# Four CA batches on VectorE and four on GpSimd, two buffers each for CA's products and for the turned E

## The chip, the cores and the metric

The kernel runs on one core of a Trainium2 chip. The metric is the device time of one execution in microseconds; the time shown is the median of three runs. The profile is of one further execution.

The core has five instruction streams that run side by side and meet at semaphores: TensorE (PE, matmuls; its weight loads are PEld), VectorE (DVE), ScalarE (ACT), GpSimd (POOL) and SyncE (SP), which here only issues DMAs. ACT issues DMAs too. Each stream executes in the order in which it was written: an instruction that waits holds back all that stands behind it on its engine.

## The reference, cut to what matters

One layer of a hybrid backbone over 512 latent tokens and 256 context tokens, all in float32. One input projection feeds three branches, which are merged by sigmoid gates and projected, and a squared-ReLU MLP follows. The change lies in branch B, a bidirectional S5 state-space layer with 32 groups of 16 channels and 64 complex states:

```
h_f = diag_scan(lam_bar[0], s5_drive(ux, b_bar[0])) + exp(lam_dt[0] * steps) * h0_f
h_b = diag_scan(lam_bar[1], flip(s5_drive(ux, b_bar[1]), 1)) + exp(lam_dt[1] * steps) * h0_b
y = real(einsum('blgp,gnp->blgn', h_f, c_mat[0]) + einsum('blgp,gnp->blgn', h_b, c_mat[1]))
y = y + d_skip * u;  g = gelu(y);  yb = (g @ w_glu_a) * sigmoid(g @ w_glu_b)
```

The kernel runs the scan over blocks of eight steps. For that it needs, per group, the input matrix times powers of lambda (the program calls it E), the output matrix times powers of lambda (CA) and the lag kernel of a block (KT). They depend on parameters only and are made at run time.

## The kernel before, in words

**Units.** The large matrices stream from HBM as 1 MB pieces `raw` through two buffers, each of which holds two halves. A half is split into a rounded part and a rest: ACT writes `wh` (L173), VectorE writes `wl` (L176). Three matmuls (L99, L100, L101) per 128 rows use them. One half is one *unit* of PE work. The units stand in a fixed list: xa, cg, xb (four each), uc (four, the context's S5 input, 256 columns), then ga, ga, cv four times, eight gb, eight gc, and then q, k, v. `slot` (L1130) takes a unit and, between its parts, pulls small pieces of the side work from generators (`pump`, L1111). A SyncE load of `raw` waits until both halves of the buffer before it are split (L144 behind L176).

**E.** `gen_s5e` (L424) makes E in eight batches of four groups. Per batch GpSimd does six TENSOR_TENSOR instructions (L422 products, L458 and L467 sums) into `e1`; PE makes the lag matmuls `kps` (L436), ACT copies them to `kev` (L437); PE turns E in `etps` (L443), ACT copies that to `et` (L445) and sends it to DRAM (E_d, L446). After the last batch SyncE writes KT_d from `kev` in 15 DMAs (L484).

**CA.** `gen_s5c` (L487) makes CA in eight batches of six instructions: two products and a difference, two products and a sum (L497 to L499; the products are in the helper `prod`, L422). Batches 0 to 4 run on VectorE, 5 to 7 on GpSimd. The result `c1` goes to DRAM by SyncE (C_d, L501). `c1` and the second product `tc` have one buffer each, the input `cb` (loaded by ACT's queue, L491) two.

**S5B.** `gen_s5b` (L720) follows when E and CA are done: its buffers lie where those of CA lay, so GpSimd's first instruction (IOTA, L618) and the first loads of `et` wait for the last C_d transfer. It has eight batches. Batch q: 32 state matmuls `stps` (L666, L667; `et` and `u` come from DRAM), VectorE rotates by `tb` (L677, L678), GpSimd combines (L683, L684), VectorE scans (L691, eight instructions) and rotates back (L697, L698), GpSimd combines `h` (L703 to L706), PE makes the output `yps` (L713, L715; needs `ks` from KT_d and `ca` from C_d), ACT copies it to `y`. `rot1` of a batch stands behind the scan of the batch before on VectorE.

**What sets the order.** The program does not fix the order of an engine by hand. The framework sorts the instructions of each engine by priority with its own timing model while the kernel is built; two pieces of code that are pumped side by side can come out interleaved. A change of buffer counts therefore moves instructions on every engine.

Of the kernel before, what the change touches and what calls it, by code (L numbers as in the profile page):

```python
# [9 lines left out]
F32 = mybir.dt.float32  # L10
# [65 lines left out]
def trunk(tc, xT, ctxT, cond, condT, vecs, wst, s5p, s5bc, dmat, biasA, outT):  # L76
# [3 lines left out]
    V, S, P, PE = nc.vector, nc.scalar, nc.gpsimd, nc.tensor  # L80
# [23 lines left out]
    with es:  # L104
# [11 lines left out]
        def pa(name):  # L116
            return pp.tile([128, 1024], F32, tag="a", bufs=2, name=name)
# [300 lines left out]
        def prod(eng, out, mat, cf, b):  # L418
            shp = [128, 4, 8, 16]
            m4 = mat[:, :, None, :].to_broadcast(shp)  # L420
            c4 = s5["CF"][cf][:, 4 * b:4 * b + 4, :, None].to_broadcast(shp)
            eng.tensor_tensor(out.rearrange("p (g s n) -> p g s n", g=4, s=8), m4, c4, op=MUL)  # L422

        def gen_s5e(pool):  # L424
            kev = pool.tile([128, 2, G, 16], F32, name="kev")

            def loadbc(b):
                t = pool.tile([128, 512], F32, tag="bc", bufs=2, name=f"bc{b}")
                nc.scalar.dma_start(t[:, 0:384], s5bc[b][:, 0:384])
                return t  # L430

            def lags(b, e1, cm):
                kps = pa(f"kps{b}")[:, :128].rearrange("p (g m) -> p g m", g=4)
                for g in range(4):
                    for c in range(2):
                        PE.matmul(kps[:, g], e1[:, c, 128 * g:128 * g + 128], cm[:, 4 * c + g], start=c == 0, stop=c == 1)  # L436
                S.copy(kev[:, :, 4 * b:4 * b + 4].rearrange("p e g m -> p g e m"), kps.rearrange("p g (e m) -> p g e m", e=2))  # L437

            def turned(b, e1):
                ps = pa(f"etps{b}").rearrange("p (a m) -> p a m", a=8)  # L440
                for g in range(4):
                    for c in range(2):
                        PE.transpose(ps[:, 2 * g + c], e1[:, c, 128 * g:128 * g + 128], ident)  # L443
                et = pool.tile([128, 8, 128], F32, tag="et", bufs=1, name=f"et{b}")
                S.copy(et, ps)  # L445
                nc.scalar.dma_start(E_d[b], et)  # L446

            bc, old = loadbc(0), None
            for b in range(9):
                if b < 8:  # L450
                    nxt = loadbc(b + 1) if b < 7 else None
                    B = bc[:, 0:128].rearrange("p (c g n) -> p c g n", c=2, g=4)
                    cm = bc[:, 128:384].rearrange("p (a m) -> p a m", a=8)
                    e1 = pool.tile([128, 2, 512], F32, tag="e1", bufs=2, name=f"e1{b}")
                    ta = pool.tile([128, 512], F32, tag="ta", name=f"ta{b}")
                    prod(P, e1[:, 0], B[:, 0], "cr", b)
                    prod(P, ta, B[:, 1], "nci", b)
                    P.tensor_tensor(e1[:, 0], e1[:, 0], ta, op=ADD)  # L458
                    yield
                if old is not None:  # L460
                    lags(b - 1, *old)
                    yield
                if b < 8:
                    ta = pool.tile([128, 512], F32, tag="ta", name=f"tb{b}")
                    prod(P, e1[:, 1], B[:, 0], "nci", b)
                    prod(P, ta, B[:, 1], "cr", b)
                    P.tensor_tensor(e1[:, 1], e1[:, 1], ta, op=SUB)  # L467
                    yield
                if old is not None:
                    turned(b - 1, old[0])  # L470
                    yield
                old = (e1, cm)
                bc = nxt

            kf0 = pool.tile([16, G, 16], F32, tag="bc", bufs=2, name="kf0")
            dmt = pool.tile([16, G, 16], F32, tag="bc", bufs=2, name="dmt")
            nc.scalar.dma_start(dmt, dmat)
            nc.sync.dma_start(kf0, kev[112:128, 0])
            yield
            V.tensor_tensor(kf0, kf0, dmt, op=ADD)  # L480
            V.tensor_tensor(kev[0:16, 1], kev[0:16, 1], kf0, op=ADD)
            for e, s in ((e, s) for s in range(8) for e in range(2) if e or s < 7):
                i = 16 * (7 * e + s)
                nc.sync.dma_start(KT_d[:, :, i:i + 16].rearrange("g n m -> n g m"), kev[16 * s:16 * s + 16, e])  # L484
            yield

        def gen_s5c(pool):  # L487
            for b in range(8):
                eng = V if b < 5 else P
                t = pool.tile([128, 128], F32, tag="cb", bufs=2, name=f"cb{b}")  # L490
                nc.scalar.dma_start(t, s5bc[b][:, 384:512])  # L491
                C = t.rearrange("p (c g n) -> p c g n", c=2, g=4)
                c1 = pool.tile([128, 2, 512], F32, tag="c1", bufs=1, name=f"c1{b}")
                yield
                for c, (x, y, o) in enumerate((("ar", "ai", SUB), ("ai", "ar", ADD))):
                    ta = pool.tile([128, 512], F32, tag="tc", name=f"tc{b}{c}")
                    prod(eng, c1[:, c], C[:, 0], x, b)  # L497
                    prod(eng, ta, C[:, 1], y, b)
                    eng.tensor_tensor(c1[:, c], c1[:, c], ta, op=o)  # L499
                    yield  # L500
                nc.sync.dma_start(C_d[b], c1)  # L501
                yield
# [660 lines left out]
        stc_cm.__exit__(None, None, None)  # L1163
        s5c_cm = tc.tile_pool(name="s5c", bufs=1, side="right")
        gcc = gen_s5c(s5c_cm.__enter__())
        gens.append(gcc)
        while ga_ in gens or gcc in gens or UNITS[i][0] != "ga":
# [306 lines left out]
```

## Time and profile before

| | |
|---|---|
| median of 3 runs | 1034.97 us (1033.2 to 1037.51) |
| profiled execution, its time | 1035.81 us |
| its span, first to last instruction | 1034.0 us (1.8 us lie around it) |
| PE busy | 993.0 us, 96% |
| DVE, ACT, POOL busy | 577.3, 379.8, 214.6 us |
| granted TensorE clock, mean | 0.982 |

[...] The page's slices show PE at 7 or 8 tenths in few places behind the start, and the clock at 8 or 9 tenths in some of the same slices.

### The profile page before, as it was taken

The numbers are of one execution on the slowest core, as the hardware profiler recorded it, in microseconds if no ns is written. First come the engines' busy times: TensorE is split into PE (matmuls) and PEld (weight loads), VectorE is DVE, ScalarE is ACT, GpSimd is POOL, SyncE is SP. The second block draws the span as 40 slices with busy tenths as digits, with TensorE's granted clock in tenths as the row PEclk, the third lists the DMA queues.
The fourth block names the chain that finished last, engine by engine and source line by source line (L and its number), as shares of the span: only waits on it lengthen the run. The fifth ranks groups of instructions, "written<-read, shape, count | busy, mean of one in ns | idle before, by whom it ended". The sixth has DMA issues, their size and how long they took to land.

```text
span 1034.0 us, 13596 instructions
## 1 busy us (share of the span) xinstructions
PE 993.0 (96%) x5386; PEld 815.8 (79%) x5386; DVE 577.3 (56%) x941; ACT 379.8 (37%) x611; POOL 214.6 (21%) x169
## 2 busy tenths in 40 slices
PE   7999997989899999999999999999999999999997
PEld 3468886778688787878877788998888888888887
DVE  4952899358781244676587895665432324443322
ACT  3234522332212233565465443444331213442311
POOL 3165654556752013310210200000000000000000
PEclk8999998999799999999999999999999999999999
DMA  9426345973547366443344574223232232232202
GB/s 367 171 95 207 124 133 194 243 253 128 173 137 223 129 246 233 137 146 107 127 144 153 190 257 151 82 84 120 82 122 82 82 119 85 82 123 82 82 1 82
DMA packets 64543, 149.38 MB, mean 144 GB/s; under 512 B 28864, under 2 KB 41152, under 8 KB 52064
## 3 DMA queue, kind: packets, MB, share of 16 engines
q1 hardware_dynamic: 47360, 137.90, 38.7%
q10 hardware_dynamic: 17120, 10.62, 3.6%
q8 instruction: 42, 0.69, 0.3%
q14 instruction: 21, 0.17, 0.0%
HBM read 130.16 MB, written 18.32 MB: 144 GB/s over the span
## 4 chain that ended last, share of the span: by engine, by line
PE 67%; DVE 13%; DMA 6%; POOL 6%; issue 3%; ACT 3%; SPq 1%; ACTq 0%; DVEq 0%; POOLq 0%
PE m L99 10%; PE m L100 10%; PE m L101 10%; DMA raw<-in_wst_dram 2%; DVE wl L176 2%; DVE v L691 2%; PE ops L846 2%; DMA C_d<-c 2%; PE wo L100 1%; PE wo L99 1%; PE wo L101 1%; PE st_a L515 1%; DVE fg L959 1%; PE ptps L831 1%; PE gc L99 1%
## 5 line engine op out<-in xcount | busy, mean ns | idle before, releaser
L176 DVE TENSOR_TENSOR wl<-raw,wh 128x1024 fp32r<-128x1024 f32 x144 | 193.6, 1344 | 218.8 <-ACT wh L173 213.9
L173 ACT CAST wh<-raw 128x1024 fp32r<-128x1024 f32 x144 | 151.1, 1050 | 300.4 <-PE m L100 151.1
L99 PE MATMUL m<-rg,wh 128*128 128x512 f32 (+1 forms) x480 | 184.2, 385 | 0.0
L101 PE MATMUL m<-rg,wl 128*128 128x512 f32 (+1 forms) x480 | 183.9, 384 | 0.0
L101 PEld LDWEIGHTS m<-rg,wl 128*128 128x128 f32 x480 | 90.1, 188 | 19.1
L99 PEld LDWEIGHTS m<-rg,wh 128*128 128x128 f32 x480 | 89.9, 188 | 18.7
L100 PE MATMUL m<-rg,wh 128*128 128x512 f32 (+1 forms) x256 | 96.4, 378 | 0.0
L1092 POOL TENSOR_TENSOR junk<-raw,silx 128x1024 f32<-128x1024 f32 x16 | 45.3, 2829 | 206.7 <-DMA raw<-in_wst_dram 198.0
L100 PE MATMUL m<-actl,wh 128*128 128x512 f32 x224 | 87.8, 392 | 0.0
L100 PEld LDWEIGHTS m<-rg,wh 128*128 128x128 f32 x256 | 48.0, 188 | 8.6
L100 PEld LDWEIGHTS m<-actl,wh 128*128 128x128 f32 x224 | 42.0, 187 | 9.8
L1047 DVE SCALAR_TENSOR_TENSOR fg<-m,mod,fg 128x512 f32<-128x512 f32 x14 | 10.5, 752 | 52.8 <-PE m L101 52.8
L691 DVE TENSOR_TENSOR_SCAN v<-r,v 128x96 f32<-128x96 f32 x64 | 29.5, 524 | 15.4 <-POOL v L683 15.4
L515 PE MATMUL st_a<-raw,cs 128*2 128x256 f32 x128 | 32.3, 407 | 5.5 <-DMA raw<-in_wst_dram 4.2
L92 ACT CAST rg<-relu 128x512 fp32r<-128x512 f32 (+1 forms) x36 | 20.3, 576 | 38.5 <-DVE relu L1040 38.5
L1096 DVE SCALAR_TENSOR_TENSOR jk<-raw,silx 128x1024 bf16<-128x1024 f32 x16 | 21.8, 1361 | 20.4 <-DMA raw<-in_wst_dram 20.3
L93 DVE TENSOR_TENSOR actl<-relu,rg 128x512 fp32r<-128x512 f32 (+1 forms) x36 | 22.3, 632 | 18.6 <-ACT rg L92 18.6
L100 PE MATMUL wo<-rg,wh 128*128 128x256 f32 (+1 forms) x104 | 31.8, 309 | 0.0
L99 PE MATMUL wo<-rg,wh 128*128 128x256 f32 (+1 forms) x104 | 31.8, 307 | 0.0
L101 PE MATMUL wo<-rg,wl 128*128 128x256 f32 (+1 forms) x104 | 31.5, 306 | 0.0
L515 PEld LDWEIGHTS st_a<-raw,cs 128*2 128x2 f32 x128 | 10.7, 89 | 24.8 <-issue 10.5
L846 PE MATMUL ops<-pt,v 128*64 128x128 f32 (+1 forms) x256 | 28.2, 293 | 1.2 <-ACT pt L833 1.2
(439 smaller groups left out, 2385.5 us busy)
## 6 DMA issues: line engine op xcount, KB each, us to landing
raw<-in_wst_dram SPq DMA_DIRECT2D x94, 1024.0 KB
E_d<-et ACTq DMA_DIRECT2D x8, 512.0 KB
C_d<-c SPq DMA_DIRECT2D x8, 512.0 KB
et<-E_d SPq DMA_DIRECT2D x8, 512.0 KB
ca<-C_d SPq DMA_DIRECT2D x8, 512.0 KB
raw<-in_wst_dram SPq DMA_DIRECT2D x4, 512.0 KB
u<-U_d SPq DMA_DIRECT2D x8, 256.0 KB
ks<-KT_d SPq DMA_DIRECT2D x32, 64.0 KB
```

The costliest lines, as they stand in the source:

```text
L92: S.copy(hi, src)
L93: (eng or V).tensor_tensor(lo, src, f(hi), op=SUB)
L99: PE.matmul(ps, a[0], b[0], start=start, stop=False)
L100: PE.matmul(ps, a[0], b[1], start=False, stop=False)
L101: PE.matmul(ps, a[1], b[0], start=False, stop=stop)
L173: S.copy(a, src)
L176: V.tensor_tensor(b, src, f(a), op=SUB)
L515: PE.matmul(ps, cs[:, kt], half(h)[:, 256 * (kt % 4):256 * (kt % 4) + 256], start=kt == 0, stop=kt == 7, skip_group_check=True)
L691: V.tensor_tensor_scan(v[:, g, c], r8, v[:, g, c], 0.0, op0=MUL, op1=ADD)
L846: PE.matmul(ops[r], v[:rows, vt, r], pt[:rows, h, t], start=t == 0, stop=t == 3, skip_group_check=True)
L1092: P.tensor_tensor(junk, half(h), silx, op=MUL)
L1096: V.scalar_tensor_tensor(jk, half(h), 1.0, silx, op0=MUL, op1=MUL, accum_out=modx[:, i:i + 1])
```

## The change

Three buffer counts and one limit. VectorE makes CA batches 0 to 3, GpSimd 4 to 7. `c1` and `tc` get two buffers each, and so does `et` in E.

```diff
@@ gen_s5e
-                et = pool.tile([128, 8, 128], F32, tag="et", bufs=1, name=f"et{b}")
+                et = pool.tile([128, 8, 128], F32, tag="et", bufs=2, name=f"et{b}")
@@ gen_s5c
-                eng = V if b < 5 else P
+                eng = V if b < 4 else P
-                c1 = pool.tile([128, 2, 512], F32, tag="c1", bufs=1, name=f"c1{b}")
+                c1 = pool.tile([128, 2, 512], F32, tag="c1", bufs=2, name=f"c1{b}")
-                    ta = pool.tile([128, 512], F32, tag="tc", name=f"tc{b}{c}")
+                    ta = pool.tile([128, 512], F32, tag="tc", bufs=2, name=f"tc{b}{c}")
```

The order on the engines follows from it. GpSimd, at the last batch of E (e_1300, ta_1301 and tb_1354 are batch 7 of E; c_1307, c_1421, c_1534 are CA batches 4, 5, 6); the rows marked + are new at their place:

```order
+L422 TENSOR_TENSOR c_1307<-cb_1305,CFar 128x512
+L422 TENSOR_TENSOR c_1307<-cb_1305,CFai 128x512
 L422 TENSOR_TENSOR ta_1301<-bc_1189,CFnci 128x512
+L422 TENSOR_TENSOR tc_1334<-cb_1305,CFai 128x512
+L422 TENSOR_TENSOR tc_1358<-cb_1305,CFar 128x512
+L499 TENSOR_TENSOR c_1307<-c_1307,tc_1334 128x512
+L499 TENSOR_TENSOR c_1307<-c_1307,tc_1358 128x512
 L422 TENSOR_TENSOR e_1300<-bc_1189,CFcr 128x512
 L422 TENSOR_TENSOR e_1300<-bc_1189,CFnci 128x512
```

Before, the six instructions of E's batch 7 stood together and CA began behind them. Now they lie among 12 products and 6 sums of CA batches 4 to 6: L458 of batch 7 comes behind the products of batch 5, L467 behind those of batch 6.

PE, at the second uc unit (uc_1426) where the lag matmuls of E's batch 7 (kps_1409) begin:

```order
-L436 MATMUL kps_1409<-bc_1189,e_1300 128x32 x3
 L99 MATMUL uc_1426<-rg_639,wh_1294 128x256
 L436 MATMUL kps_1409<-bc_1189,e_1300 128x32
 L100 MATMUL uc_1426<-rg_640,wh_1294 128x256
-L436 MATMUL kps_1409<-bc_1189,e_1300 128x32
-L101 MATMUL uc_1426<-rg_639,wl_1295 128x256
-L436 MATMUL kps_1409<-bc_1189,e_1300 128x32
-L99 MATMUL uc_1426<-rg_639,wh_1294 128x256
```

One of the eight kps stays there, behind the first matmul of the unit; the other seven, and seven of the eight etps of the batch, now stand behind the sixth matmul of the first ga unit.

PE, at the last S5B state batch (stps_2564) of the 8; before it comes in gb_2491, the first gb unit:

```order
-L100 MATMUL gb_2491<-rg_75,wh_2201 128x512
-L101 MATMUL gb_2491<-rg_73,wl_2202 128x512
-L99 MATMUL gb_2491<-rg_73,wh_2201 128x512
-L100 MATMUL gb_2491<-rg_75,wh_2201 128x512
 L666 MATMUL stps_2564<-u_2332,et_2399 64x96
 L667 MATMUL stps_2564<-u_2332,et_2399 64x96
```

```order
 L666 MATMUL stps_2564<-u_2332,et_2399 64x96
 L667 MATMUL stps_2564<-u_2332,et_2399 64x96
+L99 MATMUL ga_2272<-rg_73,wh_1980 128x512
+L100 MATMUL ga_2272<-rg_75,wh_1980 128x512
+L101 MATMUL ga_2272<-rg_73,wl_1981 128x512
+L99 MATMUL ga_2272<-rg_74,wh_1980 128x512
```

Now it comes in ga_2272, the sixth ga unit. Counted over the whole order, 512-wide matmuls from the first uc unit to the first state batch: 139 before, 111 now; from the first to the last state batch: 157 before, 138 now; from the last state batch to the end of the gb units: 184 before, 231 now.

## Rows read from the trace of the kernel before

**Rows 1.** Windows: busy time of each engine, granted clock, DMA share
```profile
60.00:160.00 100.00, 99.75 (x517) 81.08 (x516) 67.61 (x86) 36.79 (x53) 58.26 (x42) 1.00 0.45 149
160.00:187.00 27.00, 19.41 (x131) 18.41 (x130) 19.68 (x26) 9.79 (x15) 12.02 (x9) 0.87 0.67 210
187.00:222.00 35.00, 32.90 (x149) 26.11 (x149) 15.03 (x14) 12.75 (x18) 17.44 (x15) 1.00 0.85 237
222.00:300.00 78.00, 70.11 (x536) 59.67 (x532) 64.08 (x118) 21.75 (x39) 48.60 (x52) 0.91 0.51 168
352.00:1034.00 682.00, 671.42 (x3596) 562.81 (x3594) 354.49 (x538) 266.29 (x440) 45.26 (x16) 0.99 0.35 123
```

**Rows 2.** Waits of PE from 60 to 340 us: total, times, longest
```profile
PE stps L666 <- DMA u<-U_d: 4.2, 2, 4.0
PE etps L443 <- ACT et L445: 3.9, 1, 3.9
PE uc L99 <- DVE fg L962: 1.7, 1, 1.7
PE uc L101 <- DVE wl L176: 1.6, 1, 1.6
```

**Rows 3.** Timeline of VectorE, CA stage: start, us, engine, line, operation, idle before
```profile
130.46 1.54 DVE L422 TENSOR_TENSOR tc<-cb,CFai 128x512 f32<-128x512 f32 x1
135.62 0.68 DVE L422 TENSOR_TENSOR tc<-cb,CFar 128x512 f32<-128x512 f32 x1
...
141.61 1.48 DVE L176 TENSOR_TENSOR wl<-raw,wh 128x1024 fp32r<-128x1024 f32 x1
...
155.52 1.44 DVE L422 TENSOR_TENSOR c<-cb,CFar 128x512 f32<-128x512 f32 x1 [1.06 <-DMA C_d<-c]
...
163.18 1.21 DVE L176 TENSOR_TENSOR wl<-raw,wh 128x1024 fp32r<-128x1024 f32 x1
```

**Rows 4.** Timeline of PE
```profile
146.76 0.39 PE L99 MATMUL xb<-rg,wh 128*128 128x512 f32 x1
170.10 0.83 PE L436 MATMUL kps<-bc,e 128*128 128x32 f32 x6 [0.36 <-issue]
187.10 0.40 PE L99 MATMUL ga<-rg,wh 128*128 128x512 f32 x1
208.44 0.39 PE L99 MATMUL ga<-rg,wh 128*128 128x512 f32 x1
219.32 0.39 PE L99 MATMUL cv<-rg,wh 128*128 128x512 f32 x1
221.70 0.27 PE L666 MATMUL stps<-u,et 128*64 128x96 f32 x1 [0.64 <-POOL rr L654]
298.92 0.25 PE L667 MATMUL stps<-u,et 128*64 128x96 f32 x1
```

**Rows 5.** Timeline of GpSimd
```profile
161.11 1.60 POOL L467 TENSOR_TENSOR e<-e,tb 128x512 f32<-128x512 f32 x1
176.55 1.92 POOL L422 TENSOR_TENSOR tc<-cb,CFai 128x512 f32<-128x512 f32 x1 [13.84 <-ACT rg L92]
218.25 0.21 POOL L618 IOTA iot<- 128x96 int32 x1 [5.14 <-DMA C_d<-c]
```

**Rows 6.** GpSimd's instructions by line: ns minimum/median/maximum
```profile
L499 POOL TENSOR_TENSOR c<-c,tc x6: 1285/1294/2269, 182.1 to 211.8; 128x512 f32<-128x512 f32 x6
L422 POOL TENSOR_TENSOR e<-bc,CFnci x8: 1062/1504/2046, 51.6 to 156.4; 128x512 f32<-128x512 f32 x8
```

**Rows 7.** Timeline of SyncE's DMA issues
```profile
187.38 7.50 SPq L484 DMA_DIRECT2D KT_d<-kev  x7
213.14 0.32 SPq L501 DMA_DIRECT2D C_d<-c  x1
...
261.88 0.33 SPq L144 DMA_DIRECT2D raw<-in_wst_dram  x1
262.31 0.38 SPq L637 DMA_DIRECT2D u<-U_d  x1
```

## The prediction

> **What bounds the kernel now.** I read the page first: PE is busy 96% of the span, so every other engine counts only where PE waits for it. Then the windows. From 60 to 160 us PE is busy without a hole. From 160 to 187 it works 19.4 of 27 us at a granted clock of 0.87, from 187 to 222 32.9 of 35 at 1.00, from 222 to 300 70.1 of 78 at 0.91; behind 352 only 10.6 of 682 us are idle, and the change does not reach there [rows 1]. So what can be won lies between 160 and 300: 7.6, 2.1 and 7.9 us of idle time, and a lower clock that costs about 0.13 x 27 = 3.5 and 0.09 x 78 = 7.0 us. Some 28 us in all. [...]
>
> Then the list of PE's waits names the causes [rows 2]. Early, three belong to CA and E: 1.7 us for L962 and 1.6 us for a `wl`, both queued on VectorE behind CA products, and 3.9 us for the `et` copy of E's batch 6, which ACT makes late because an instruction ahead of it waits for the same VectorE queue. Later, 4.2 us for `u` in S5B, nearly all in one wait of 4.0: SyncE could issue that `u` only at 262.31, right behind a `raw` load at 261.88 that had to wait for its buffer [rows 7].
>
> The third reading is GpSimd's. Its E is finished at 161.11 + 1.60 = 162.7; then it idles 13.8 us for a CA buffer and begins CA at 176.55; S5B's first instruction, IOTA, comes at 218.25, 5.1 us behind the last C_d issue at 213.14 [rows 5, 7]. PE makes the first state matmul at 221.70, 3.45 us behind IOTA, and the last at 298.92 [rows 4].
>
> **How I count.** S5B is a loop over eight batches whose order on PE is fixed, so the end of the affected part is: start of the first `stps`, plus the time from first to last `stps` (77.2 us before), plus the matmul work that stands behind the last one. Behind that work nothing in the order differs. One 512-wide matmul follows the next in (219.32 - 208.44) / 48 = 0.227 us; 48 matmuls lie between these two rows [rows 4].
>
> **Part 1: work left behind S5B.** In the new order 231 instead of 184 wide matmuls stand behind the last `stps`, 47 x 0.227 = +10.7 us. This is the price of starting S5B earlier: 28 fewer stand ahead of it (6.4 us) and 19 fewer within (4.3 us).
>
> **Part 2: VectorE's four batches.** Batch 4 leaves VectorE, six instructions of 0.68 us beside an idle GpSimd and up to 1.54 beside a busy one [rows 3], and the waits for C_d go (one was 1.06 us at 155.52). But with two buffers the scheduler puts batches 0 to 3 closer together and further forward: ahead of the `wl` of the third xb unit stand 15 CA instructions where 7 stood. That `wl` ended at 141.61 + 1.48 = 143.1, PE began the unit at 146.76 and needs it 0.5 us later [rows 3, 4]. Eight more instructions cost 5.4 us (0.68) to 12.3 us (1.54), so it ends between 148.5 and 155.4; GpSimd is idle for part of the stretch, so I take 150.7, a new PE wait of 3.5 us where there was none. What PE loses here it no longer loses at the first uc unit (1.7 + 1.6), since the `wl` there, at 163.18, has six more CA instructions ahead of it (4.1 us) and fewer waits (1.06 and the bubbles between dependent neighbours): about 164.5.
>
> **Part 3: GpSimd and the lag matmuls of E's batch 7.** Now GpSimd's CA instructions stand among the six of E's last batch. Two of its `tc` products need buffers that VectorE's batch 3 frees just before that `wl`, so GpSimd goes on at about 164. From there to L458, for which the first kps waits, are 7 products and 3 sums: 7 x 1.06 + 3 x 1.29 = 11.3 us at the shortest durations, 7 x 1.50 + 3 x 1.60 = 15.3 us at those beside a busy VectorE [rows 5, 6]. L458 ends between 175.3 and 179.3; VectorE is half idle then, so I take 176.5. PE comes to this kps at about 170, as before [rows 4], and everything of uc_1426 but one matmul stands behind it. So PE waits 6.5 us; the 3.9 us for `et` fall away, because its second buffer and the shorter VectorE queue have it copied meanwhile. L467, for which the other seven kps wait, has 5 products and 3 sums more: 184.5 to 191.6.
>
> PE reaches the first ga matmul at 187.1 - (1.7 + 1.6 + 3.9) + 3.5 + 6.5 = 189.9; I leave the clock's loss as it was, since the waits add up to more but lie apart. (The kps and etps that move behind ga's sixth matmul come off ahead of it.) Six matmuls later, at 191.3, the lag matmuls are done: PE, not GpSimd, decides that. Bounds: 186 (no new wait at all) to 200 (GpSimd at its long durations and late with its buffers).
>
> **Part 4: the start of S5B.** Behind the kps come the `kev` copy (0.7 us), 14 KT_d issues of 7.50 / 7 = 1.07 us on SyncE [rows 7], that is 15.0, then one `raw` and the last C_d (0.7), 5.1 us until IOTA and 3.45 until `stps`: 25.0 us together. KT_d now stands ahead of the last C_d, so this chain, not GpSimd's CA (which ends some 10 us behind L467), sets the start: 191.3 + 25.0 = 216.3, 5.4 us earlier than 221.70. Queued behind KT_d on SyncE are a `raw` load that PE needs only two units later, and S5B's `et`, `u`, `ca`, `ks`.
>
> **Part 5: the loop.** 77.2 us before for 7 steps, 11.0 each. From below: VectorE is busy 64.1 of the 78 us [rows 1]; with no hole the loop would take 0.82 x 77.2 = 63.4. From PE: 19 wide matmuls fewer and all else equal give 77.2 - 4.3 = 72.9. From above: VectorE's and GpSimd's hand-overs set the pace whatever PE has to do: 77.2. Fewer `wl` and gate instructions lie between the scans now, and the 4.0 us for `u` shrink since its `raw` is one load earlier; but PE has less work to lay over the hand-overs. I take 70, -7.2 us, between the first two and nearer the second.
>
> **The sum.** -5.4 - 7.2 + 10.7 = -1.9 us, against the profiled execution's own 1035.81 us. The median of the runs is 0.84 us lower; I subtract from it: 1034.97 - 1.9 = 1033.1.
>
> **The rivals.**
> *The loop becomes short.* With VectorE at its floor, 64 us, and S5B at 215: -6.7 - 13.2 + 10.7 = -9.2, 1025.8. For it: in the loop PE now has to wait for VectorE rather than the reverse, and its 82% leave room. Against it: the scan needs GpSimd's sums, which need VectorE's products. It is faster by over 0.5% from a loop under some 66.5 us.
> *The loop keeps its pace* (77.2): -5.4 + 10.7 = +5.3, 1040.3. For it: GpSimd, busy 48.6 of 78 us, and VectorE alternate [rows 1]. Against it: the 4.0 us were SyncE's fault, not theirs.
> *Slower: E's batch 7 comes late.* GpSimd runs beside VectorE at 1.50 to 1.60 us an instruction and waits for `cb` and `c1`, so that L467 ends at 197 and the kps at 198. Then S5B starts at 223.0, +1.3; with the loop at 72.9 that is +1.3 - 4.3 + 10.7 = +7.7, 1042.7. It decides from a kps end of 195.5 on. For it: GpSimd waited 13.8 us for a buffer before [rows 5]. Against it: there are now two.
> [...]
>
> **Chances.** Forecast 0.42 (own range 1029.5 to 1037), short loop 0.25, loop as before 0.14, late batch 7 0.19. Range for 8 in 10: 1025 to 1042. Faster by over 0.5% (5.2 us, about what can be told from no change here) 0.30, within 0.46, slower 0.24: the loop as before lies on the border, and the forecast has a small tail on the fast side.
>
> **What would show it.** Right: PE waits about 3 us for a `wl` in the third xb unit, and 6 us in the second uc unit at a kps, with L458 as releaser; no wait of 3.9 at etps; IOTA near 213, the first `stps` near 216, the last near 286. Wrong: no wait at that kps (then all comes some 6 us earlier and rival one gains), a wait at the seven kps in ga, a loop of 77, or a new wait behind the S5B stage.

## The result: slower by 1.2%

| | before | changed |
|---|---|---|
| median of the runs, us | 1034.09 (1032.35 to 1037.51, 4 runs) | 1050.01 (1046.4 to 1050.47, 4 runs) |
| profiled execution, us | 1035.81 | 1050.32 |
| its span, us; mean granted clock | 1034.0; 0.982 | 1048.5; 0.966 |

The ratio on record is 1.0119, with a 95% interval of 1.0081 to 1.0157; the two medians of the table alone, four runs each, give 1.0154, still inside it. I had forecast 1033.1, with 1025 to 1042 as the range; the measured time lies outside it.

Windows of the changed kernel's trace, over the stretches of [rows 1] (PE, PEld, DVE, ACT, POOL busy, granted clock as a share of full speed, DMA share, GB/s):

```profile
60.00:160.00 100.00, 95.52 (x477) 75.92 (x476) 66.90 (x91) 36.94 (x53) 52.00 (x37) 0.97 0.43 146
160.00:187.00 27.00, 18.92 (x114) 17.38 (x113) 14.67 (x15) 7.70 (x11) 25.93 (x19) 0.81 0.53 178
187.00:222.00 35.00, 32.71 (x176) 27.95 (x174) 11.62 (x12) 12.29 (x19) 18.57 (x16) 1.00 0.87 215
222.00:300.00 78.00, 68.98 (x496) 58.68 (x498) 66.09 (x116) 21.51 (x40) 50.64 (x53) 0.84 0.54 181
352.00:1048.50 696.50, 683.36 (x3648) 572.45 (x3646) 356.76 (x540) 269.64 (x445) 44.62 (x16) 0.99 0.35 123
```

Compare the column of the clock with [rows 1]. From 222 to 300 PE is busy almost as long as before (69.0 against 70.1 us), but at 0.84 instead of 0.91. The first stretch, which had no hole, now has 4.5 us of them and a clock of 0.97.

The waits of PE in the changed kernel (us in total, times, longest), as [rows 2]:

```profile
PE kps L436 <- POOL e L458: 8.1, 1, 8.1
PE stps L666 <- DMA u<-U_d: 3.5, 2, 2.8
PE stps L666 <- issue: 3.4, 1, 3.4
PE yps L713 <- DMA ks<-KT_d: 2.3, 2, 1.1
PE xb L101 <- DVE wl L176: 2.2, 1, 2.2
PE xb L99 <- DVE fg L956: 2.0, 1, 2.0
```

The waits of [rows 2] at uc and etps are gone, and three new ones stand in their place: twice VectorE in the xb units, once GpSimd at the lag matmuls.

The same in PE's timeline (start, us, engine, line, operation, idle before):

```profile
150.32 0.47 PE L99 MATMUL xb<-rg,wh 128*128 128x512 f32 x1 [2.02 <-DVE fg L956]
153.24 0.79 PE L101 MATMUL xb<-rg,wl 128*128 128x512 f32 x1 [2.21 <-DVE wl L176]
181.08 0.63 PE L436 MATMUL kps<-bc,e 128*128 128x32 f32 x2 [8.08 <-POOL e L458]
222.51 0.27 PE L666 MATMUL stps<-u,et 128*64 128x96 f32 x1 [2.80 <-DMA u<-U_d]
292.46 0.39 PE L666 MATMUL stps<-u,et 128*64 128x96 f32 x1 [3.37 <-issue]
301.30 0.37 PE L667 MATMUL stps<-u,et 128*64 128x96 f32 x1
```

The row of xb L101 lasts 0.79 us, where the one at 147.21 lasts 0.39, and that of kps 0.63, where the pair at 146.30 lasts 0.30: what follows these two waits runs slowly, at a granted clock of 0.50 until 158 and until 185 (windows of 1 us; it is 1.00 at both of the earlier rows).

To add this up, I cut each trace into windows of 2 us (20 us behind 370) and took from each the idle time (length less PE busy) and the time lost to the clock (PE busy x (1 - granted clock)). All accounts below are made so, "idle / clock" in us:

| | 0 to 60 | 60 to 210 | 210 to 370 | behind | sum |
|---|---|---|---|---|---|
| before | 10.2 / 3.1 | 9.3 / 3.2 | 10.9 / 6.0 | 10.6 / 3.2 | 41.0 / 15.6 |
| changed | 9.1 / 5.3 | 12.6 / 4.9 | 12.7 / 13.1 | 11.7 / 4.2 | 46.1 / 27.6 |

Of the 14.5 us of span, 5.1 are idle time and 12.0 the clock; the two together are 2.6 too many, and the work that remains in the sum differs by that (977.3 against 974.8); no row shows why. The first column differs though nothing was changed there: the clock's share varies by some us between executions (3.1 and 5.3 us here). From 60 to 370 alone, where the change acts, it is 5.1 us of idle time and 8.8 of clock: most of the loss is no wait at all but what follows the waits.

### The profile page after: what moved, and what is told of

Its sections match the earlier page's. It is cut to its first block, busy times and chain, and to the rows that moved or that the text cites. A ratio compares the mean times of both kernels' runs of the same rounds, so it can differ in the third digit from the quotient of the medians.

```text
span 1048.5 us, 13592 instructions
## 1 busy us (share of the span) xinstructions
PE 1002.3 (96%) x5386; PEld 823.8 (79%) x5386; DVE 572.5 (55%) x935; ACT 379.6 (36%) x611; POOL 223.9 (21%) x175
## 4 chain that ended last, share of the span: by engine, by line
PE 70%; DVE 11%; DMA 6%; POOL 5%; ACT 2%; issue 2%; SPq 1%; ACTq 0%; DVEq 0%; POOLq 0%
PE m L99 10%; PE m L100 10%; PE m L101 10%; DMA raw<-in_wst_dram 3%; DVE v L691 2%; PE ops L846 2%; PE wo L100 1%; PE wo L99 1%; DVE wl L176 1%; PE wo L101 1%; PE gb L99 1%; PE gb L100 1%; PE gb L101 1%; PE st_a L515 1%; PE ptps L831 1%
## 5 line engine op out<-in xcount | busy, mean ns | idle before, releaser
L176 DVE TENSOR_TENSOR wl<-raw,wh 128x1024 fp32r<-128x1024 f32 x144 | 190.2, 1321 | 233.1 <-ACT wh L173 228.6
L173 ACT CAST wh<-raw 128x1024 fp32r<-128x1024 f32 x144 | 151.0, 1050 | 308.9 <-PE m L100 151.1
L101 PE MATMUL m<-rg,wl 128*128 128x512 f32 (+1 forms) x480 | 183.9, 384 | 0.0
L101 PEld LDWEIGHTS m<-rg,wl 128*128 128x128 f32 x480 | 90.1, 188 | 19.1
L1047 DVE SCALAR_TENSOR_TENSOR fg<-m,mod,fg 128x512 f32<-128x512 f32 x14 | 10.5, 750 | 52.8 <-PE m L101 52.8
L1096 DVE SCALAR_TENSOR_TENSOR jk<-raw,silx 128x1024 bf16<-128x1024 f32 x16 | 23.9, 1496 | 21.1 <-DMA raw<-in_wst_dram 21.1
L93 DVE TENSOR_TENSOR actl<-relu,rg 128x512 fp32r<-128x512 f32 (+1 forms) x36 | 22.3, 630 | 18.5 <-ACT rg L92 18.5
L101 PE MATMUL wo<-rg,wl 128*128 128x256 f32 (+1 forms) x104 | 31.5, 306 | 0.0
L515 PEld LDWEIGHTS st_a<-raw,cs 128*2 128x2 f32 x128 | 10.8, 90 | 24.7 <-issue 10.8
L436 PEld LDWEIGHTS kps<-bc,e 128*128 128x128 f32 x128 | 21.6, 193 | 10.6 <-POOL e L458 8.3
```

Source lines behind the costliest of these rows:

```text
L93: (eng or V).tensor_tensor(lo, src, f(hi), op=SUB)
L101: PE.matmul(ps, a[1], b[0], start=False, stop=stop)
L173: S.copy(a, src)
L176: V.tensor_tensor(b, src, f(a), op=SUB)
L515: PE.matmul(ps, cs[:, kt], half(h)[:, 256 * (kt % 4):256 * (kt % 4) + 256], start=kt == 0, stop=kt == 7, skip_group_check=True)
L1096: V.scalar_tensor_tensor(jk, half(h), 1.0, silx, op0=MUL, op1=MUL, accum_out=modx[:, i:i + 1])
```

## The experiments

Each ratio compares with 13 to 31 runs of the kernel before, made beside the experiment's own on the same chip, where before took 1037.9 to 1039.7 us. The accounts are of one execution each, and not always of a typical one: that of hold took 1034.39 us (its median is 1038.03), that of limit_only 1051.08 (its median is 1043.37; it was the slowest of ten).

| kernel | ratio to before (95%) | idle / clock 60 to 210 | 210 to 370 |
|---|---|---|---|
| hold | 0.9991 (0.9962 to 1.0019) | 8.4 / 4.5 | 9.6 / 7.9 |
| buffers_only | 0.9989 (0.9959 to 1.0019) | 9.8 / 9.1 | 9.5 / 5.5 |
| limit_only | 1.0072 (1.0039 to 1.0105) | 11.7 / 4.0 | 11.8 / 12.3 |
| six_on_vector | 1.0099 (1.0062 to 1.0135) | 11.1 / 6.4 | 13.7 / 9.3 |
| hold_limit | 0.9997 (0.9970 to 1.0024) | 8.0 / 3.4 | 10.5 / 7.4 |
| et_only | 0.9994 (0.9967 to 1.0021) | 9.0 / 3.7 | 10.2 / 9.5 |
| fill_kps | 1.0282 (1.0237 to 1.0327) | 20.1 / 4.7 | 12.3 / 9.7 |
| fill_u | 1.0022 (0.9999 to 1.0045) | 8.3 / 3.2 | 10.8 / 5.5 |
| one_hole | 1.0214 (1.0154 to 1.0275) | 8.4 / 3.2 | 9.4 / 5.8 |
| six_holes | 1.0292 (1.0233 to 1.0350) | 8.5 / 3.7 | 9.7 / 8.5 |
| eighteen_holes | 1.0174 (1.0113 to 1.0234) | 8.2 / 4.2 | 8.8 / 10.2 |
| u_on_act | 1.0007 (0.9975 to 1.0040) | 8.2 / 3.3 | 10.5 / 4.8 |
| ks_ca_two | 0.9999 (0.9978 to 1.0020) | 8.2 / 4.3 | 12.3 / 8.1 |
| ks_ca_two_u | 1.0012 (0.9988 to 1.0035) | 8.9 / 3.2 | 11.5 / 9.2 |
| hold_ks_ca_two_u | 1.0014 (0.9987 to 1.0040) | 7.9 / 4.1 | 15.9 / 6.6 |
| after_ks_ca_two_u | 1.0152 (1.0120 to 1.0185) | 12.6 / 5.0 | 16.3 / 11.4 |

et_only and the three kernels with holes (whose edits act behind 700 us) have before's order up to 370 us, and their clock's share from 210 to 370 lies between 5.8 and 10.2. Before's 6.0 is at the low end of that and the changed kernel's 13.1 outside it.

### Which part of the change costs

**hold.** GpSimd's CA stays behind E:

```diff
-                    P.tensor_tensor(e1[:, 1], e1[:, 1], ta, op=SUB)
+                    order["e", b] = P.tensor_tensor(e1[:, 1], e1[:, 1], ta, op=SUB)
...
+                while eng is P and ("e", 7) not in order:
+                    yield
...
+                    with after(("e", 7)) if eng is P else nullcontext():
+                        prod(eng, c1[:, c], C[:, 0], x, b)
```

> The changed kernel, but GpSimd's products of CA batches 4 to 7 are held behind the last instruction of E (L467 of batch 7), so that they can't stand between E's. All buffers stay as changed. Theory A (new waits of TensorE in front of S5B, each followed by a stretch at the lower clock, made the loss): the 8.1 us wait at kps goes, and some 3 us of lower clock behind it; the waits for VectorE in the xb units (2.0 and 2.2 us) stay, since VectorE's order is the same. 1050 - 11 = about 1039 us. Theory B (the S5B loop takes 77 to 79 us however few matmuls lie in it, and what is left behind it is the price): 208 wide matmuls stay behind the last stps instead of 231, 5 us less; about 1045 us whatever happens to kps.

The time is that of before. The wait at kps is gone, and so are 5.2 us of the clock's loss in S5B. With the batches and buffers of the change, and CA's order on VectorE too, the whole loss went: it came from where GpSimd's CA stands. Theory B's 1045 was wrong. Theory A had the cause, but its 1039 us came by luck: it was counted from 1050, where before took 1034, and so meant a ratio of about 1.005. More came back than the 11 us that it had.

**buffers_only.** On the changed kernel:

```diff
-                eng = V if b < 4 else P
+                eng = V if b < 5 else P
```

> All three buffer counts as changed, but five batches on VectorE as before. The order on the engines: 117 wide matmuls from uc to the first stps, 142 in the loop, 220 behind it (changed kernel 111, 138, 231; before 139, 157, 184). GpSimd's first sum of E's batch 7 stands ahead of all CA products, its second behind six of them. Theory A: no wait at the first kps, at most 2 us at the seven others, the 4 us for VectorE in the xb units with their lower clock stay: 1036 to 1040 us. Theory B: 36 more wide matmuls than before behind a loop that keeps its 77 us, +8 us, less what an earlier start gives back (0 to 5): 1038 to 1043, and the loop's length tells it: 77 us or more by B, about 73 by A.

The same time as before, with 220 wide matmuls left behind the loop, which took 73.3 us (223.44 to 296.78): theory A was right in the time and in the loop. Its waits at kps are 2.1 and 1.3 us. But one wait in S5B is as long as that at kps in the changed kernel:

```profile
PE yps L713 <- DMA ks<-KT_d: 8.1, 1, 8.1
```

Its idle time from 210 to 370 is still only 9.5 us, since the other waits there are gone. So one long wait need not make a kernel slower; the sum has to be taken.

**limit_only.** On the kernel before:

```diff
-                eng = V if b < 5 else P
+                eng = V if b < 4 else P
```

> Four batches on VectorE, all buffers as before. The order: 161 wide matmuls from uc to the first stps, 140 in the loop, 178 behind. VectorE's order around the third xb unit is that of before. Theory A: no wait in xb, none at kps over 1 us, the 3.3 us at the first uc units shrink: 1030 to 1035 us. Theory B: start 22 x 0.227 = 5 us later, loop 77 us although 17 wide matmuls fewer lie in it, 1 us less behind: 1037 to 1039 us.

Slower by 0.7%: theory A's 1030 to 1035 was wrong because I had looked at VectorE's order and not at GpSimd's. Theory B's loop of 77 us was wrong too, it took 70.7 (232.38 to 303.04). GpSimd's timeline in limit_only:

```profile
158.90 1.72 POOL L458 TENSOR_TENSOR e<-e,ta 128x512 f32<-128x512 f32 x1
169.75 1.91 POOL L422 TENSOR_TENSOR tc<-cb,CFai 128x512 f32<-128x512 f32 x1 [9.13 <-ACT rg L92]
171.63 1.50 POOL L422 TENSOR_TENSOR tb<-bc,CFcr 128x512 f32<-128x512 f32 x1
173.21 2.12 POOL L467 TENSOR_TENSOR e<-e,tb 128x512 f32<-128x512 f32 x1
```

One CA product (`tc`) waits 9.1 us, and E's last product and sum, which need nothing that it waits for, stand behind it. PE then waited 5.1 us at kps for that L467.

**hold_limit.** limit_only with the edit of hold.

> Four batches on VectorE with all buffers as before, and GpSimd's CA held behind the last instruction of E. Without the hold this took 1.0072 of before, with waits of 1.9 and 5.1 us at kps and 4.0 us of lower clock behind them. In its order one CA product stood ahead of E's last product and sum on GpSimd. Theory A (that one product, waiting for its buffer in an in-order queue, makes the kps late): both waits go with their clock, 9 to 11 us less: ratio 0.996 to 0.999. Rival (four batches on GpSimd with one buffer are too slow in themselves, S5B starts at 232 and its loop keeps 70 to 77 us): ratio 1.004 to 1.008.

0.9997, as theory A had it. The same place on GpSimd:

```profile
163.13 1.39 POOL L422 TENSOR_TENSOR tb<-bc,CFcr 128x512 f32<-128x512 f32 x1
164.60 1.60 POOL L467 TENSOR_TENSOR e<-e,tb 128x512 f32<-128x512 f32 x1
173.39 1.92 POOL L422 TENSOR_TENSOR tc<-cb,CFai 128x512 f32<-128x512 f32 x1 [7.20 <-ACT rg L92]
```

The product still waits, 7.2 us, but now behind E, where nothing of E is queued. Twice, then, the hold alone takes a slower kernel back to the time of before.

**six_on_vector.** On the changed kernel:

```diff
-                eng = V if b < 4 else P
+                eng = V if b < 6 else P
```

> All buffers as changed, but six batches on VectorE and two on GpSimd, which stand behind E. The order: 110 wide matmuls from uc to the first stps, 137 in the loop, 232 behind, nearly the numbers of the changed kernel. Theory A: no wait at kps; the waits for VectorE's wl in the xb units stay and come again at uc, 6 to 9 us with 3 us of lower clock: 1037 to 1042 us. Theory B: as the changed kernel, 1047 to 1050 us, since border and loop are the same.

Slower by 1%, without CA among E's instructions on GpSimd: theory A's number was wrong, and theory B's 1047 to 1050 us came (1047.3; the ratio is near that of the changed kernel, and the loop took 76.8 us, 221.94 to 298.71). PE waits 3.1 and 1.6 us in the xb units, 3.1 at etps, and in S5B 3.7 for ks and 2.7 for `h`; its clock's loss in S5B is 9.3. So the order on GpSimd is not the only way to lose 10 us here. Whether theory B's reason is the right one for it is not shown, and why its S5B loses more than that of buffers_only, with 137 instead of 142 wide matmuls in the loop, is left open.

**et_only.** On the kernel before:

```diff
-                et = pool.tile([128, 8, 128], F32, tag="et", bufs=1, name=f"et{b}")
+                et = pool.tile([128, 8, 128], F32, tag="et", bufs=2, name=f"et{b}")
```

> The kernel before with two buffers for E's et alone. The order on all engines is word for word that of before. By the prediction's Part 3 the second buffer helps the 3.9 us wait of etps for the et copy; theory now: that copy is late only because ACT stands behind an rg that VectorE delays (L962), so the wait stays at 3 to 4 us and the ratio is 1.000 within 0.003. Rival: the wait goes with its 1.7 us of clock, 5 us, ratio 0.995.

```profile
PE etps L443 <- ACT et L445: 4.1, 1, 4.1
```

ACT's timeline, in the same kernel:

```profile
177.11 0.62 ACT L92 CAST rg<-fg 128x512 fp32r<-128x512 f32 x1 [5.15 <-DVE fg L962]
177.63 1.00 ACT L445 COPY et<-etps 128x1024 f32<-128x1024 f32 x1
```

The wait stays: the second buffer is worth nothing here, as the copy waits for its turn on ACT, behind an `rg` that waits 5.2 us for VectorE, and not for a buffer.

### What a wait of PE costs

**fill_kps.** On the changed kernel, in `lags`:

```diff
+                if b == 7:
+                    with after(("mm", ("uc", 0), False)), tc.tile_critical():
+                        for _ in range(9):
+                            PE.matmul(kp_[:, 512:1024], ident, f(RG[0])[:, 0:512], start=True, stop=True)
```

> The changed kernel with nine idle matmuls (128x128 by 128x512 in float32, into an unused half of the lag matmuls' PSUM tile) put on TensorE behind the first matmul of the second uc unit, where it waits 8.1 us for L458. All other engines keep the order of the changed kernel, nothing is taken away. [...] Rival C (the clock falls for another reason, such as the load so far): 0.50 from 181 to 186 all the same, and the time of the changed kernel or up to 1 us more. The rows of the clock at 181 to 187 decide.

The nine matmuls were to keep PE busy in the wait of 8.1 us; by theory A the clock would then stay at 1.00 behind it and the time come to 1047 to 1048.5 us (an estimate from the 2.2 us of clock lost there). The fill missed its aim: the block of idle matmuls waited itself, for GpSimd's `tb`, and took 10 us from there:

```profile
188.98 9.98 PE L439 MATMUL kps<-rg,ident 128*128 128x512 f32 x18 [15.28 <-POOL tb L423]
```

It answers another question, though: behind this wait of 15.3 us the clock's loss was 1.9 us, against 2.2 behind the 8.1 us of the changed kernel.

**fill_u.** On the kernel before, in S5B's `states`:

```diff
+                if q == 5:
+                    with after(("mm", ('ga', 7), True)), tc.tile_critical():
+                        for _ in range(16):
+                            PE.matmul(ps_[:, 384:512], ident, ident, start=True, stop=True)
```

> The kernel before with 16 idle matmuls (128x128 by 128x128 in float32, into unused columns of the state tile) on TensorE ahead of the sixth state batch, where it waited 4.0 us for u at 264.0 and then ran at 0.50 from 268 to 280, a loss of 5.9 us. Nothing else moves but the output matmuls of batch 2, which the scheduler puts ahead of that state batch. Theory A: the matmuls take 3.4 us inside the wait, the clock stays at 1.00 behind it: 4 to 6 us faster than the kernel before, ratio 0.994 to 0.996. Rival C: 0.50 behind it all the same; ratio 1.000.

It missed in the same way: the block waited 4.7 us for GpSimd, and 0.50 followed. Neither fill kept PE busy, so neither tells theory A from rival C.

**one_hole, six_holes, eighteen_holes.** Artificial waits in the MLP; only the units and NHOLE (17, 2, 0) differ:

```diff
+            if UNITS[i] in HOLES:
+                hp = pss(f"hole{i}")
+                with tc.issue_after(last_mm[0].ins):
+                    PE.matmul(hp[:, 0:32], ident, ident[:, 0:32], start=True, stop=True)
+                V.tensor_copy(junk[:, 0:32], hp[:, 0:32])
+                for _ in range(NHOLE):
+                    P.tensor_tensor(junk[:, 0:512], junk[:, 0:512], junk[:, 0:512], op=SUB)
+                with tc.issue_after(last_mm[0].ins):
+                    order["gate"] = PE.matmul(hp[:, 32:64], ident, junk[:, 0:32], start=True, stop=True)
...
+            with after("gate"):
+                mm_unit(UNITS[i], False)
```

> The kernel before with one artificial wait of TensorE in the MLP (unit m1 12, a stretch at 1.00 without a hole): a small matmul, a VectorE copy, 17 GpSimd subtractions of 128x512 one behind the other (about 1.06 us each) and a small matmul that needs the last of them; TensorE's later work is held behind that. Nothing is taken away. The wait is about 18.5 us. [...] Rival C (a hole costs its length alone): +18.5, 1.018; the clock behind it stays at 1.00.

> As one_hole, but six waits of about 3 us (two GpSimd subtractions each) at six units of the MLP, 16 us or more apart; together 18 us, as much as the one wait of one_hole. [...] Rival C: +18, ratio 1.017, as one_hole.

> As one_hole, but 18 waits of about 1 us (no GpSimd step, only matmul, VectorE copy, matmul) at 18 units of the MLP; together some 18 us. In the kernel before, holes of 1.0, 1.1, 1.2 and 1.4 us were followed by no lower clock. Theory A with that: +18 to +22 us, ratio 1.017 to 1.021; were a hole of 1 us as dear as one of 3, +50 to +100.

The medians stand 22.5, 30.7 and 18.5 us above those of before. The wait of one_hole was 19.7 us, those of six_holes 2.9 each, 17.5 together; so six waits with less idle time in all cost more than one (the slowest run of one_hole, 1062.75, lies below the fastest of six_holes, 1065.63), and most of the rest is clock. Windows of one_hole (the wait, and behind it):

```profile
735.00:758.00 23.00, 3.65 (x18) 2.92 (x16) 3.46 (x4) 2.16 (x3) 17.72 (x17) 0.64 0.14 46
758.00:761.00 3.00, 2.69 (x7) 2.25 (x8) 0.00 (x0) 0.00 (x0) 0.25 (x1) 0.50 0.00 0
761.00:764.00 3.00, 3.00 (x13) 2.45 (x12) 0.00 (x0) 1.08 (x2) 0.00 (x0) 0.88 0.00 0
764.00:767.00 3.00, 3.00 (x15) 2.49 (x14) 2.31 (x3) 1.08 (x2) 0.00 (x0) 1.00 0.00 0
```

Windows of six_holes (its first wait, at 710, and its second, at 730):

```profile
710.00:713.00 3.00, 0.14 (x2) 0.03 (x1) 1.63 (x2) 0.62 (x1) 2.40 (x2) 1.00 0.82 279
713.00:716.00 3.00, 2.95 (x14) 2.50 (x15) 0.00 (x0) 0.00 (x0) 0.00 (x0) 1.00 0.20 76
730.00:733.00 3.00, 0.11 (x1) 0.00 (x0) 1.61 (x2) 0.62 (x1) 2.40 (x2) 0.87 0.00 0
733.00:736.00 3.00, 2.98 (x8) 2.50 (x9) 0.00 (x0) 0.00 (x0) 0.00 (x0) 0.50 0.00 0
736.00:739.00 3.00, 3.00 (x8) 2.32 (x8) 0.00 (x0) 0.45 (x1) 0.00 (x0) 0.50 0.00 0
```

In 3 us PE makes 14 or 15 matmuls at 1.00 and 8 at 0.50. The clock's loss behind the six waits was 0, 3.0, 1.5, 1.6, 0 and 2.9 us, 9.0 in all; behind the one long wait 1.7; behind the 18 short ones (18.5 / 18 = 1.0 us each, of which the trace shows 0.4 as a wait and the rest as ends of the two small matmuls) nothing, the clock from 700 to 950 is 1.00. So rival C is wrong. Theory A is right in kind. It had put 2 to 6 us of clock behind each wait, an estimate from the 1.9 us in fill_kps, 2.2 in the changed kernel and 5.9 in the kernel before, which made +20 to +24 us for one_hole and +30 to +54 for six_holes. That is too much for the MLP: equal waits cost between 0 and 3 us of clock there. Four of the six waits were followed by a stretch at 0.50, two by no fall; in all they cost 9.0 us of clock against 1.7 for one.

### What paces the S5B loop

**u_on_act.** On the kernel before, in `loadu`:

```diff
-                nc.sync.dma_start(u, U_d[q // 2].rearrange("s (n h g) m -> (s n) h g m", n=16, h=2)[:, q % 2])
+                nc.scalar.dma_start(u, U_d[q // 2].rearrange("s (n h g) m -> (s n) h g m", n=16, h=2)[:, q % 2])
```

> The kernel before with the eight loads of u issued from ScalarE's queue instead of SyncE's, where the fifth stood behind a raw load that waited for its buffer. TensorE's order is that of before but for one matmul. In the profile of before the wait for that u was 4.0 us and 5.9 us of lower clock followed. Theory A: both go, up to 10 us, if nothing else is late: ratio 0.990 to 0.995. Rival (the next thing is late at the same place, ks or VectorE's hand-over, and the hole stays with its clock): ratio 0.998 to 1.003.

```profile
PE yps L713 <- DMA ks<-KT_d: 7.4, 4, 3.8
```

No wait for `u` is left, but one of 3.8 us for ks stands at 261 to 265, and 4.8 us of clock follow. The rival is right: the next load was late at the same place.

**ks_ca_two, ks_ca_two_u, hold_ks_ca_two_u, after_ks_ca_two_u.**

```diff
-                ca = self.tl("ca", q, [128, 2, 4, 128], bufs=1)
+                ca = self.tl("ca", q, [128, 2, 4, 128], bufs=2)
...
-                ks = self.tl("ks", q, [128, 4, 128], bufs=1)
+                ks = self.tl("ks", q, [128, 4, 128], bufs=2)
```

> The kernel before with two buffers for ks and ca in S5B instead of one. In its order 105 wide matmuls lie between the first and the last stps (157 before) and 235 behind (184). Theory L (loads pace the loop): no ks or ca wait in S5B, the loop takes 62 to 66 us, with at most one lower-clock stretch; ratio 0.988 to 0.996. Theory H (the hand-over of VectorE and GpSimd paces it): with 52 wide matmuls (11.8 us) fewer in it the loop still takes 70 us or more, the difference stands as holes with stps or yps waiting for DVE or POOL, each with its lower clock; ratio 1.003 to 1.015.

> As ks_ca_two, and the loads of u on ScalarE's queue. 113 wide matmuls in the loop, 227 behind. Theory L: as ks_ca_two without its u wait, ratio 0.986 to 0.994. Theory H: ratio 1.000 to 1.012, holes for DVE or POOL.

> The changed kernel with GpSimd's CA held behind E, two buffers for ks and ca and u on ScalarE's queue: 138 wide matmuls from uc to the first stps, 113 in the loop, 252 behind. The hold alone took 0.9991 of before. Theory L: 0.986 to 0.994, a version that beats both. Theory H: 1.000 to 1.012.

> The changed kernel with two buffers for ks and ca and u on ScalarE's queue; 111 wide matmuls to the first stps, 96 in the loop, 272 behind. The wait at kps (8.1 us and its clock) stays. Theory L: S5B's share of the loss goes (3 us of idle, 7 of clock): ratio 1.000 to 1.004 against before. Theory H: 1.010 to 1.020.

The first three are the kernel before in time, the last one the changed kernel: no version beat before. PE's waits in ks_ca_two:

```profile
PE yps L715 <- POOL h L705: 6.3, 4, 2.8
PE yps L715 <- POOL h L706: 2.3, 2, 1.1
```

The loads hardly hold PE up any more (0.6 us for ks, 1.2 for et); GpSimd's `h`, the end of the hand-over with VectorE, does. The loop took 223.78 to 286.25, 62.5 us, which is theory L's figure, but with theory H's waits, and nothing was won, as 52 more wide matmuls (11.8 us) stand behind it and the idle time from 210 to 370 rose from 10.9 to 12.3. Theory L's ratios all missed. Theory H's came in the last three, and its 1.003 to 1.015 for ks_ca_two lies above the measured interval.

after_ks_ca_two_u and hold_ks_ca_two_u differ by the edit of hold alone, so they test it a third time: 1.0152 against 1.0014. The slower of the two has the shorter loop (60.9 us against 62.5) with fewer wide matmuls in it (96 against 113); the wait of 8.1 us at kps is in the one and not in the other. So the hold does not win by bringing matmuls back into the loop.

## Why the prediction was wrong, step by step

In the terms of its sum: the start of S5B came at +0.8 us against before where -5.4 was forecast, the loop at +1.6 for -7.2, the work left behind at +11.0 for +10.7; another 1.1 came behind it. That is 14.5 us instead of -1.9. In the reading ahead of the sum the clock's cost was put a little high: a share of PE's busy time is lost and not of the span, so 0.13 x 19.4 = 2.5 and 0.09 x 70.1 = 6.3 us, not 3.5 and 7.0.

**Right: VectorE's earlier CA (Part 2).** 3.5 us in the third xb unit were forecast, 2.0 + 2.2 came, one for `fg` (L956) and one for the `wl`, and the waits at uc went.

**Right in place, short in size: the lag matmuls (Part 3).** The wait at the first kps of uc_1426, with L458 as releaser, was to be 6.5 us and was 8.1. GpSimd in the changed kernel:

```profile
161.07 1.76 POOL L422 TENSOR_TENSOR c<-cb,CFar 128x512 f32<-128x512 f32 x1 [10.16 <-DMA C_d<-c]
...
166.26 1.50 POOL L422 TENSOR_TENSOR tc<-cb,CFai 128x512 f32<-128x512 f32 x1
...
179.76 1.26 POOL L458 TENSOR_TENSOR e<-e,ta 128x512 f32<-128x512 f32 x1
...
190.97 2.27 POOL L467 TENSOR_TENSOR e<-e,tb 128x512 f32<-128x512 f32 x1
...
217.75 0.21 POOL L618 IOTA iot<- 128x96 int32 x1 [14.46 <-DMA C_d<-c]
```

A CA product waits 10.2 us for a buffer of `c1`, and E's batch 7 stands behind it. That wait cost E little, for its own input `bc` was loaded late as well. ACT's issue of that load in the changed kernel:

```profile
157.10 0.33 ACTq L429 DMA_DIRECT2D bc<-in_s5bc_dram  x1
```

The same load, and the instruction that needs it, in hold:

```profile
154.77 0.34 ACTq L429 DMA_DIRECT2D bc<-in_s5bc_dram  x1
157.37 3.14 POOL L422 TENSOR_TENSOR ta<-bc,CFnci 128x512 f32<-128x512 f32 x1 [8.79 <-DMA bc<-in_s5bc_dram]
```

In hold 2.6 us passed from issue to use; with that, batch 7 could not have begun here before about 159.7 (an estimate), 1.4 us ahead of the CA product. What made L458 late is the work: of the 20.0 us from 161.07 to its end, ten CA instructions took 13.2 and E's own four 6.8. L458 ended at 181.0, beyond my 175.3 to 179.3; L467 at 193.2, beyond my 191.6. GpSimd came to the first of its `tc` products at 166.26 where I had 164, and from there to the end of L458 it took 181.0 - 166.3 = 14.8 us, not the 12.5 that I took. I had counted 7 products and 3 sums there; the timeline has 8 and 3, which makes my bounds 12.4 and 16.8. PE came to the kps at 173.0 and not at 170, so its wait grew by less than L458 was late. That the second `et` buffer takes the 3.9 us away was wrong (et_only): that wait was merely overtaken by the one at kps. In hold, which has the second buffer and no wait at kps, 2.4 us of it stand again.

**Wrong: "I leave the clock's loss as it was, since the waits add up to more but lie apart."** This is the step that failed by most: a term put at nothing. The clock's loss grew by 12.0 us of the 14.5, 1.7 from 60 to 210 and 7.1 from 210 to 370. The reason given was upside down: waits that lie apart can each bring a slow stretch of their own (9.0 us of clock behind the six of six_holes against 1.7 behind the one of one_hole). Its size is not settled to better than some us: 2.2 of the 12.0 lie before the change begins and 1.0 behind it, and the five executions in before's own order lost 5.8 to 10.2 us in S5B, 8.0 on average, so that only 5.1 of the 7.1 lie beyond that average.

**Wrong: the start of S5B (Part 4), forecast 216.3, measured 222.51.** The lag matmuls were done at 195, not at 191.3. Then came what the chain of Part 4 did not hold. ACT in the changed kernel (ACTq is its DMA issue):

```profile
194.36 4.12 ACTq L968 DMA_DIRECT2D U_d<-uc_sb  x1
...
199.53 0.26 ACT L437 COPY kev<-kps 128x128 f32<-128x128 f32 x1
```

The `kev` copy, for which I had 0.7 us, came 4 us late, because ACT was still issuing DMAs of U_d until 198.5 and made one `wh` (1.05 us) first. On SyncE:

```profile
200.48 9.12 SPq L484 DMA_DIRECT2D KT_d<-kev  x14
...
210.59 0.36 SPq L501 DMA_DIRECT2D C_d<-c  x1
...
218.15 0.79 SPq L637 DMA_DIRECT2D u<-U_d  x2
```

The 14 issues took 9.1 us where I had 15.0, but the last C_d took 7.2 us to release IOTA instead of 5.1, and `u` was issued only behind `et`, so PE waited another 2.8 us. Before, four loads of `u` had gone ahead of the last C_d (213.14):

```profile
205.21 1.77 SPq L637 DMA_DIRECT2D u<-U_d  x4
```

Against the chain of Part 4 that makes 3.8 us for the late kps, 4.0 for `kev`, -4.9 from there to the last C_d, 2.1 to IOTA and 1.3 to the first stps, 6.3 in all. They gave back the 5.4 us that an earlier start was to bring.

**Wrong: the loop (Part 5), forecast 70 us, measured 222.51 to 301.30, 78.8.** Its idle time is 8.5 us against 7.9 before, its clock's loss 11.3 against 6.1 (windows of 1 us). The longest wait, the row with "issue", looks like the hand-over: the state batch at 292.46 follows VectorE's last rotation of an earlier batch, and the program has two such PSUM buffers (L117). The profile names no releaser, so this is my reading:

```profile
291.58 0.54 DVE L678 TENSOR_TENSOR B<-stps,tb 128x384 f32<-128x384 f32 x1
```

That ends at 292.12. The other waits in the loop are mostly for loads (ks 2.3, et 1.4, u 0.7 us). With 19 wide matmuls fewer the waits did not become fewer, and the clock fell three times from 222 to 306 where before it fell once: behind the wait for `u` at the start (3.9 us lost), behind 0.7 and 1.1 us of waits from 263 to 266 (3.4) and behind this hand-over (5.9); before, 6.0 behind the 4.0 us for `u`. Without the 5.2 us more of clock the loop would have been 73.6 us, near the 72.9 that I had for "19 fewer and all else equal".

**Right as a sum, wrong as a price: the work left behind (Part 1).** From the last stps to the first gc matmul it is 301.7 to 365.66, 64.0 us, against 299.2 to 352.22, 53.0, before: +11.0, forecast +10.7. But ks_ca_two moves 11.8 us behind the loop at no cost. All of PE's work has to be done, and what counts is idle time and clock.

**The rivals.** The late batch 7 had the start (223.0) and the sign, with the kps done at 195.1, a hair short of its 195.5; the loop that keeps its pace had the loop (77.2). I had put them up as alternatives, with 0.19 and 0.14. They do not exclude each other: +1.3 and +10.7 give 1047, within 3 us of what came.

**Left open.** Why S5B's clock falls for longer where E is late. The number of wide matmuls in the loop is not the reason: hold (157), buffers_only (142), hold_ks_ca_two_u (113) and ks_ca_two (105) lose nothing. The four kernels with a late E (the changed one, limit_only, after_ks_ca_two_u, fill_kps) lost 13.1, 12.3, 11.4 and 9.7 us of clock from 210 to 370, all others 4.8 to 10.2, so the two ranges overlap at their ends. And six_on_vector (137) is 1% slower with no CA among E's instructions, for a reason that no run here singles out.

## What to carry to other kernels

When a change moves work to another in-order engine, look for what unrelated work the scheduler has put behind it. Count both what stands ahead of that work (13.2 us of CA in the changed kernel) and the first moved instruction that can wait (9.1 us for one product in limit_only); holding the moved work behind it won back here all that was lost, three times. Count the matmul engine's time as work, idle time and clock, and give new waits a price beyond their length: here 0 to 3 us each for equal ones in dense matmuls, and up to 5.9 in S5B. Rivals that act in different stages have to be added, not weighed against each other.

## What the runs showed of the hardware

Equal waits of 2.9 us in the MLP were followed by losses of 0 to 3.0 us of clock, at a granted clock of 0.50 (six_holes); one of 19.7 us by 1.7 (one_hole), and 18 of about 1 us by none (eighteen_holes, 1.00 from 700 to 950). So neither the idle time in all nor the number of waits alone gives the clock's price: six waits, 17.5 us together, cost more clock (9.0 us) than the one of 19.7, and eighteen short ones cost none. In the changed kernel two waits that lay close together (2.0 and 2.2 us in the xb units) were followed by a stretch at 0.50, from 152 to 158, and so were the 0.7 and 1.1 us between 263 and 266 in S5B, from 268 to 274.
